# A gated attention block on one core: x loaded with its features in the partitions, norm factors spread by four transposes, first queries and keys tile by tile of u

## The chip, the cores and the metric

The kernel runs on one core of one Trainium2 chip. The metric is the device time of one execution in microseconds (us). PE stands for TensorE, DVE for VectorE, ACT for ScalarE, POOL for GpSimd and SP for SyncE, as in the profile; line numbers such as L157 are those of the kernel before, if nothing else is said.

## What is computed

One layer of a block with three branches on x (512 tokens, 1024 features), with 256 memory tokens and a feed-forward part of 4096 columns, all float32:

```
u = rmsnorm(x, g_mix)
proj = u @ w_in          # GLA q,k,v,out-gate,alpha | FoX q,k,v,forget | memory query | 3 gates
y_gla, y_fox, y_mem = three attentions, each through its output matrix
h = x + (sig(g0)*y_gla + sig(g1)*y_fox + sig(g2)*y_mem) @ w_out
h = h + square(relu(rmsnorm(h, g_ffn) @ w_ff1)) @ w_ff2
out = rmsnorm(h, g_final)
rmsnorm(x, g): x * rsqrt(mean(x*x over the features) + 1e-6) * g
mk, mv = split(rmsnorm(mem, g_mem) @ w_mem_kv)
```

u is needed with its features in the partitions: 8 tiles of 128 features by 512 tokens. The mean runs over the features.

## The kernel before

Every factor of a product is split in two parts, a high one (`whi`, `uhi`: the value cast to a rounded 32-bit type) and a low one (`wlo`, `ulo`: what the cast left off), and a product is three matmuls: high by high, high by low, low by high (`mm3`, L157 to L159). The weights lie in DRAM as chunks of 128 x 1024 (512 KB). For a chunk, SP issues the load into one of three buffers `raw`, ACT casts it to `whi` (L147), DVE subtracts to get `wlo` (L148), in `split_w`; `whi` and `wlo` have three buffers each as well. PE runs in the order of the program text. What ACT, DVE, POOL and SP do is put in order by a scheduler when the kernel is built, within what explicit "after" relations leave open; once built, each engine runs its instructions strictly in that order.

POOL issues two kinds of DMA that matter here. `next_sum` (L122) counts the calls of `split_w`; from the 12th call on it issues with each call one step that makes sums of weight chunks in DRAM (tiles `T`: copies at L133, adding transfers at L131), and each step waits for the cast of its call. The two gate projections of the second half (`gate_group`) work on sums of weight chunks too: `wb` buffers are loaded by SP, and a second chunk is added by a POOL DMA (`plus`, L1032); then ACT casts the buffer (L147), DVE takes the low part (L148), and eight groups of three matmuls on 128x256 follow (`product`). `take` brings the product out of PSUM: for number 5 it is an ACT copy into `ct` (L1062).

The front, before the change: x comes as four tiles of 128 tokens by 1024 features (`xn`). For each, ACT squares it with a running sum (L330), DVE and POOL make the norm factor (L333, and a power of -0.5 on POOL, L334), and DVE scales the tile (L340). PE has meanwhile computed the memory keys (L380) and half of the memory values (`mem_values`, L394). It then transposes x, 32 blocks of 128x128 (L408), eight blocks of four at a time into PSUM, with the rest of the memory values between them. ACT makes `uhi` (L411) and DVE `ulo` (L412) of each tile, both from PSUM. After it come `g_proj` (L504/L505, the projection with the alpha and forget columns, 16 matmuls) and `fox_pair(0)`: the first 128 query columns (24 matmuls) and then the first 128 key columns (24 matmuls), whose `ulo` and low weights are all there by then.

Of the kernel before, what the change touches and what calls it, by code (L numbers as in the profile page):

```python
# [9 lines left out]
F32 = mybir.dt.float32  # L10
# [7 lines left out]
P = 128  # L18
D = 1024
S = 512  # L20
# [12 lines left out]
def chunk_list():  # L33

    L = []
    for c in (0, 512):
        L += [("N", "w_mem_kv", 2 * j, c) for j in range(4)]
    L += [("G",)]
    L += [("T", "w_in", OFF["fq"]), ("T", "w_in", OFF["fk"])]
# [24 lines left out]
def hybrid_block(ctx, tc, chunks, wst, memT, xN, gffn, gfin, wup, cst, out):  # L64
# [57 lines left out]
    def next_sum(after):  # L122
# [5 lines left out]
        for to, src, add_ in islice(sums[len(late_on)], 1 + (len(late_on) == 1)):  # L128
            with tc.issue_after(merged[0]) if late_on else ExitStack():
                if add_:  # L130
                    d = nc.gpsimd.dma_start(to, src, accum_op=ALU.add, max_dma_last_dim=8192)  # L131
                else:
                    d = nc.gpsimd.dma_start(to, src)  # L133
            tc.add_manual_dep(d.ins, after.name, mybir.DependencyInfo(mybir.DependencyClass.Sync, mybir.DependencyReason.DATA),
                              reason="pace")

# [116 lines left out]
    with pool("front") as fp:  # L253
# [4 lines left out]
        xn = fp.tile([P, NT, D], F32, name="xn")  # L258
        ssx = small(fp, NT, "ssx")
# [61 lines left out]
        load, act, vec = next(lead(chunks[4], after=(load, act, vec)))  # L321

        def x_load(t):
            with behind(load):
                return nc.sync.dma_start(xn[:, t, :], xN[t * P:(t + 1) * P, :]).ins

        def x_square(t):
            sq = fp.tile([P, D], F32, tag="xsq", name=nm("xsq"), bufs=2)
            with behind(act):
                a = nc.scalar.activation(sq, xn[:, t, :], AF.Square, accum_out=ssx[:, t:t + 1]).ins  # L330
            ms, r = (fp.tile([P, 1], F32, tag=g, name=nm(g), bufs=2) for g in ("ms", "rr"))
            with behind(vec):
                m = nc.vector.tensor_scalar(ms, ssx[:, t:t + 1], 1.0 / D, EPS, op0=ALU.mult, op1=ALU.add).ins  # L333
            nc.gpsimd.tensor_tensor(r, ms, mhalf[:, :1], op=ALU.pow)  # L334
            return a, m, r

        def x_scale(t, r, cols=(0, D)):
            for sl in (slice(a, b) for a, b in zip(cols, cols[1:])):
                with behind(vec):
                    v = nc.vector.tensor_scalar(xn[:, t, sl], xn[:, t, sl], r, None, op0=ALU.mult).ins  # L340
            return v

        for t in range(2):
            load = x_load(t)
            act, vec, r = x_square(t)
            if t == 0:
                vec = x_scale(t, r)
        load, act, vec = next(lead(chunks[5], after=(load, act, vec)))
        load = x_load(2)
        act, vec, r2 = x_square(2)  # L350
        vec = x_scale(1, r)
        vec = x_scale(2, r2)
        load = x_load(3)
        act, vec, r = x_square(3)
        x_scale(3, r, (0, 2 * P, D))
        x_act = act
        with behind(load):
            nc.sync.dma_start(ident, cst[:, :P])
        get_plain = get_w

        def get_first(key):
            return pre[key] if key in pre else get_plain(key)

        get_w = get_first
# [18 lines left out]
        def mem_values():  # L383
            pss = [at_() for _ in range(2)]
            for j in range(4):
                with behind(u_mid if j == 3 else None):
                    w = [x.rearrange("p (k c) -> p k c", k=2) for x in get_w(("N", "w_mem_kv", 2 * j, 512))]
                for low in range(2):
                    for t, ps in enumerate(pss):
# [6 lines left out]
                        if j == 3 and low:  # L396
                            with tc.issue_after(u_end):
                                nc.vector.tensor_copy(gqT[t], ps)
                        yield

        def k_copies(after, hs):
            with tc.issue_after(after):
                for h in hs:
                    nc.scalar.copy(mk_raw(h), kps[h])

        def turn(pt, k, ts):
            for t in ts:
                nc.tensor.transpose(pt[:, t * P:(t + 1) * P], xn[:, t, k * P:(k + 1) * P], ident)  # L408

        def u_split(pt, k):  # L410
            a = nc.scalar.mul(uhi[:, k, :], pt, gmix[:, k:k + 1]).ins  # L411
            return a, nc.vector.scalar_tensor_tensor(ulo[:, k, :], pt, gmix[:, k:k + 1], f(uhi[:, k, :]), op0=ALU.mult,  # L412
                                                  op1=ALU.subtract).ins
# [3 lines left out]
        k_copies(x_act, (0, 1))  # L417
        mv = mem_values()
        macc, rm, dg = gv[:, 2, :M], gv[:, 1, :2], gv[:, 3, :M]
        msq = [fp.tile([P, 4, M], F32, name=f"msq{h}") for h in range(2)]  # L420
        u_act = None
        run(islice(mv, 8))
        pts, u_mid = [at_() for _ in range(2)], None
        for ts in (range(NT - 1), (NT - 1,)):
            for k in range(2):
                turn(pts[k], k, ts)
        for k in range(KT):
            if k > 1:
                pts.append(at_())
                turn(pts[k], k, range(NT))  # L430
            u_act, u_end = u_split(pts[k], k)
            u_mid = u_act if k == 3 else u_mid
            u_late = u_act if k <= 5 else u_late
            if k in (1, 3, 5):
                run(islice(mv, 2))
            if k in (5, 7):
                h = k // 7
                with tc.issue_after(u_act):
                    nc.scalar.activation(msq[h], memr[:, 4 * h:4 * h + 4, :], AF.Square)
        k_copies(u_act, (2, 3))  # L440
        run(mv)
        hold[0] = u_late
        get_w = get_plain
        g_raw = wp.tile([P, 1024], F32, tag="raw", name=nm("raw"))
        with tc.issue_after(nc.sync.dma_start(g_raw, wst[index["G",]]).ins):
            nc.sync.dma_start(cst_s[:, P:5 * P], cst[:, P:5 * P])
            nc.sync.dma_start(wup_s, wup)
            nc.sync.dma_start(cmask, cst[:, 5 * P:])

        with tc.issue_after(u_end):  # L450
            nc.vector.tensor_copy(msk_s.rearrange("p a b -> p (a b)"), cst_s[:, 3 * P:5 * P])
            nc.vector.tensor_tensor(msq[0], msq[0], msq[1], op=ALU.add)
            nc.vector.tensor_tensor(msq[0][:, :2, :], msq[0][:, :2, :], msq[0][:, 2:, :], op=ALU.add)
            nc.vector.tensor_tensor(macc, msq[0][:, 0, :], msq[0][:, 1, :], op=ALU.add)
# [31 lines left out]
    with pool("fox") as xp:  # L486
        gaT = xp.tile([P, S], F32, tag="oT", name="gaT")
        def ga_evac(ps):
            nc.scalar.copy(gaT, ps)
            nc.vector.memset(gaT[32:33, :], 1.0)  # L490
# [4 lines left out]
        def g_proj():  # L495

            raw = g_raw.rearrange("p (k c) -> p k c", k=KT)
            w = wp.tile([P, 1024], F32R, tag="hi", name=nm("whi")).rearrange("p (k c) -> p k c", k=KT)
            with tc.issue_after(hold[0]):
                nc.scalar.copy(w, raw)  # L500
            nc.vector.tensor_tensor(w[:, :, 64:], raw[:, :, 64:], f(w[:, :, 64:]), op=ALU.subtract)
# [6 lines left out]
        g_proj()  # L508
# [58 lines left out]
        def fox_pair(j):  # L567
# [12 lines left out]
            yield from proj(OFF["fq"] + P * j, q_evac)  # L580
            yield from proj(OFF["fk"] + P * j, k_evac)
# [104 lines left out]
        run(fox_pair(0))  # L686
# [581 lines left out]
    with pool("ff") as yp:  # L1268
# [51 lines left out]
        @contextmanager  # L1320
        def in_order():

            traced = nc.cur_bb.bb.instructions
            last, behind = traced[-1], {}
            yield
            for i in traced[next(k for k in reversed(range(len(traced))) if traced[k] is last) + 1:]:
                if i.engine in (mybir.EngineType.DVE, mybir.EngineType.Activation, mybir.EngineType.SP):
                    if i.engine in behind:
                        tc.add_manual_dep(i, behind[i.engine].name, mybir.DependencyInfo(
                            mybir.DependencyClass.NoSync, mybir.DependencyReason.DATA), reason="order")  # L1330
                    behind[i.engine] = i

# [360 lines left out]
def layout(inputs):  # L1693
# [39 lines left out]
    def tl(a):  # L1733
# [26 lines left out]
        "wst": wst, "memT": mem_flat, "xN": np.ascontiguousarray(x),  # L1760
# [27 lines left out]
```

## Time and profile before

| | |
|---|---|
| median of 3 runs | 815.94 us (815.68 to 816.97) |
| profiled execution | 815.5 us, of which the profiled span is 813.7 us |
| granted TensorE clock, mean | 0.997 |
| PE busy | 803.3 us (99%) |
| DVE, ACT, POOL busy | 591.3, 442.0, 109.0 us |

The span runs from the first to the last instruction that the profiler saw; 1.8 us of the profiled execution's time lie outside it. In the lists, a row has the start in us, the duration in us, the engine, the line, the operation, output <- inputs, the size, and in brackets how long the engine had been idle and what released it. "x2" is a row of two instructions of one kind, which the duration spans.

### The profile page before, as it was taken

Reading aid. Unit: us, or ns where it says so; the run is one execution under the profiler, and the core shown is the slowest. Engines: PE = TensorE matmul, PEld = TensorE weight load, DVE = VectorE, ACT = ScalarE, POOL = GpSimd, SP = SyncE. Lnnn points to the kernel's source line nnn. Section 1 sums busy time; section 2 is a strip of 40 time slices with the busy share of each in tenths; the row PEclk is TensorE's granted clock in tenths of the full one; section 3 lists DMA queues with packets and bytes.
Section 4 is the critical chain, followed back from the end, with each engine's and each line's share of the span. In section 5 each row is a group of like instructions: output and inputs, shape, how many; then the busy total and the mean of one; then the engine's idle time right before and its main releaser. Section 6 shows DMA issues by size and latency. Waiting matters only on the chain.

```text
span 813.7 us, 12505 instructions
## 1 busy us (share of the span) xinstructions
PE 803.3 (99%) x4813; PEld 706.9 (87%) x4813; DVE 591.3 (73%) x913; ACT 442.0 (54%) x699; POOL 109.0 (13%) x135
## 2 busy tenths in 40 slices
PE   8999999999999999999999999999999999999996
PEld 7788888888888888999999889987998899889984
DVE  5856878546455587877567468788788778887896
ACT  7745655543344334444454346874676367637764
POOL 0000110011101112134144110011001100100011
PEclk9999999999999999999999999999999999999998
DMA  9534666688888877767768733998758966896643
GB/s 354 168 118 139 190 177 200 184 236 200 252 236 273 232 227 184 170 165 196 199 148 225 247 98 130 279 233 232 239 163 200 222 210 167 194 281 193 160 82 125
DMA packets 39484, 161.29 MB, mean 198 GB/s; under 512 B 4736, under 2 KB 5184, under 8 KB 37056
## 3 DMA queue, kind: packets, MB, share of 16 engines
q0 software_dynamic: 9776, 58.20, 34.3%
q1 hardware_dynamic: 27856, 97.55, 34.1%
q10 hardware_dynamic: 1792, 4.75, 1.7%
q8 instruction: 37, 0.61, 0.3%
q14 instruction: 23, 0.19, 0.1%
HBM read 158.35 MB, written 35.68 MB: 238 GB/s over the span
## 4 chain that ended last, share of the span: by engine, by line
PE 92%; DVE 3%; ACT 2%; DMA 2%; issue 1%; POOL 0%; POOLq 0%; DVEq 0%; ACTq 0%
PE mm L1233 18%; PE mm L157 17%; PE mm L158 17%; PE mm L159 17%; PE a L157 5%; PE a L158 4%; PE a L159 4%; PE mm L380 1%; PE a L394 1%; DMA b<-in_wst_dram 1%; ACT hi L1357 1%; DVE lo L1291 1%; PE a L624 1%; DVE h L1285 1%; PE a L662 1%
## 5 line engine op out<-in xcount | busy, mean ns | idle before, releaser
L148 DVE TENSOR_TENSOR wlo<-raw,whi 128x1024 fp32r<-128x1024 f32 x65 | 84.1, 1296 | 58.4 <-ACT whi L147 58.2
L157 PE MATMUL mm<-uhi,whi 128*128 128x512 f32 (+1 forms) x352 | 125.8, 357 | 0.0
L159 PE MATMUL mm<-uhi,wlo 128*128 128x512 f32 (+1 forms) x352 | 123.7, 351 | 0.0
L158 PE MATMUL mm<-ulo,whi 128*128 128x512 f32 (+1 forms) x352 | 123.6, 351 | 0.0
L147 ACT CAST whi<-raw 128x1024 fp32r<-128x1024 f32 x65 | 68.4, 1052 | 89.2 <-PE mm L158 54.4
L1289 ACT CAST hi<-raw 128x1024 fp32r<-128x1024 f32 x56 | 58.8, 1050 | 45.1 <-PE mm L1233 30.2
L1291 DVE TENSOR_TENSOR lo<-raw,hi 128x1024 fp32r<-128x1024 f32 x56 | 68.5, 1223 | 14.6 <-ACT hi L1289 14.6
L157 PEld LDWEIGHTS mm<-uhi,whi 128*128 128x128 f32 x352 | 66.7, 189 | 9.9 <-issue 1.5
L159 PEld LDWEIGHTS mm<-uhi,wlo 128*128 128x128 f32 x352 | 66.6, 189 | 9.1
L158 PEld LDWEIGHTS mm<-ulo,whi 128*128 128x128 f32 x352 | 66.7, 189 | 8.1
L1233 PE MATMUL mm<-u2l,hi 128*128 128x256 f32 x240 | 66.1, 283 | 0.0
L1233 PE MATMUL mm<-u2h,hi 128*128 128x256 f32 x240 | 66.1, 283 | 0.0
L1233 PE MATMUL mm<-u2h,lo 128*128 128x256 f32 x240 | 61.1, 283 | 0.0
L1643 POOL DMA_DIRECT2D b<-in_wst_dram x30 | 25.6, 854 | 264.2 <-DVE lo L1291 153.3
L1289 ACT CAST hi<-b 128x1024 fp32r<-128x1024 f32 x36 | 37.8, 1049 | 38.1 <-PE mm L159 24.0
L158 PE MATMUL mm<-lo,ch 128*128 128x512 f32 x136 | 53.0, 390 | 0.7 <-DVE lo L1291 0.7
L157 PE MATMUL mm<-hi,ch 128*128 128x512 f32 x136 | 52.9, 389 | 0.0
L159 PE MATMUL mm<-hi,cl 128*128 128x512 f32 x136 | 52.9, 389 | 0.0
L1233 PE MATMUL mm<-u2sh,hi 128*128 128x256 f32 x192 | 52.6, 283 | 0.0
L1233 PE MATMUL mm<-u2sl,hi 128*128 128x256 f32 x192 | 52.5, 283 | 0.0
L1291 DVE TENSOR_TENSOR lo<-b,hi 128x1024 fp32r<-128x1024 f32 x36 | 43.9, 1221 | 10.4 <-ACT hi L1289 10.2
L1233 PE MATMUL mm<-u2sh,lo 128*128 128x256 f32 x192 | 47.5, 283 | 0.0
(423 smaller groups left out, 2105.7 us busy)
## 6 DMA issues: line engine op xcount, KB each, us to landing
raw<-in_wst_dram SPq DMA_DIRECT2D x113, 512.0 KB
raw<-T SPq DMA_DIRECT2D x32, 512.0 KB
b<-in_wst_dram POOLq DMA_DIRECT2D x32, 512.0 KB, 5.6
T<-in_wst_dram POOLq DMA_DIRECT2D x12, 1024.0 KB, 9.0
b<-in_wst_dram SPq DMA_DIRECT2D x16, 512.0 KB
wb<-in_wst_dram POOLq DMA_DIRECT2D x15, 512.0 KB, 5.4
T<-in_wst_dram POOLq DMA_DIRECT2D x12, 512.0 KB, 5.7
wb<-in_wst_dram SPq DMA_DIRECT2D x8, 512.0 KB
```

The source lines that it names most:

```text
L147: cast = nc.scalar.copy(hi, raw)
L148: low_now[0] = nc.vector.tensor_tensor(lo, raw, f(hi), op=ALU.subtract).ins
L157: nc.tensor.matmul(ps, lh, rh, start=start, stop=False, skip_group_check=on)
L158: nc.tensor.matmul(ps, lh, rl, start=False, stop=False, skip_group_check=on)
L159: nc.tensor.matmul(ps, ll, rh, start=False, stop=stop, skip_group_check=on)
L380: nc.tensor.matmul(kps[h], w[:, h * P:(h + 1) * P], x[:, k, :], start=k == p == 0, stop=k == KT - 1 and p == 2)
L394: nc.tensor.matmul(ps, x[:, k, sl], w[low][:, kk, :], start=k == low == 0 and x is mxh, stop=k == KT - 1 and low == 1)
L624: nc.tensor.matmul(ps[e], q[a, sl], k[a, :w], start=p == 0, stop=p == 2)
L1233: nc.tensor.matmul(ps[:, a, :], x[:, a, k, :], y[:, s, k, :], start=start, stop=stop, skip_group_check=go is not None)
L1289: nc.scalar.copy(hi, raw)
L1291: nc.vector.tensor_tensor(lo, raw, f(hi), op=ALU.subtract)
L1643: nc.gpsimd.dma_start(to[i], wst[index["B", q, i, x]], accum_op=ALU.add)
```

## The change

- x is given a second layout in DRAM, `xT`: four pieces of 2 x 128 features by 512 tokens, so that SP loads it with the features in the partitions (`xt`). The 32 transposes go away.
- The squares are made on ACT from `xt` and added up over the eight feature tiles by DVE. Four matmuls with a column of ones sum over the partitions, giving the mean for 128 tokens each; one power on POOL makes all 512 factors (`rx`); four transposes, each of a column spread over 128 columns, put them as the same row in all partitions in PSUM (`rb`), and ACT copies that into SBUF (`rb_s`).
- The tiles of `xt` are multiplied by that row: tiles 0, 1 on DVE from `rb`, tiles 2 and 4 on DVE from `rb_s`, tiles 3, 5, 6, 7 on POOL from `rb_s`. `uhi` (ACT) and `ulo` (DVE) are made from `xt` in SBUF.
- The memory values come ahead of the first use of u. Then the first queries and keys go tile by tile of u: four matmuls for a tile (high weights of both by `uhi` and `ulo`), then `g_proj`, then the 16 matmuls of the low weights.
- The weights for them are loaded earlier (their order: the first queries, the first keys, then the chunk of `g_proj`), and they, like memory-value chunks 6 and 7, are split without a call of `next_sum`. The instructions of ACT, DVE and SP in the front are held in the order of the text (`in_order`, moved up in the file). The copies of the memory values to `gqT` go from DVE to ACT.

The core of the diff:

```diff
+        def x_square(j):
+            sq = fp.tile([P, 2, S], F32, tag="xsq", name=nm("xsq"), bufs=3)
+            for k in range(2) if j == 3 else [slice(0, 2)]:
+                nc.scalar.activation(sq[:, k], xt[:, 2 * j:2 * j + 2, :][:, k], AF.Square)
+            if j == 1:
+                nc.vector.tensor_tensor(sq, sq, sqs[0], op=ALU.add)
+            sqs.append(sq)
...
+        def lead_w(key, raw):
+            hi, lo = pre[key] = [wp.tile([P, 1024], F32R, tag=g, name=nm(g)) for g in ("hi", "lo")]
+            nc.scalar.copy(hi, raw)
+            return lambda: nc.vector.tensor_tensor(lo, raw, f(hi), op=ALU.subtract)
...
-        run(islice(mv, 8))
-        pts, u_mid = [at_() for _ in range(2)], None
-        for ts in (range(NT - 1), (NT - 1,)):
-            for k in range(2):
-                turn(pts[k], k, ts)
+        lead_w(chunks[6], vraws[0])()
+        run(islice(mv, 9))
+        ps = at_()
+        for t in range(NT):
+            nc.tensor.matmul(ps[:, t:t + 1], ssum[:, t * P:(t + 1) * P], ones[:, 0:1], start=True, stop=True)
+        nc.vector.tensor_scalar(ms, ps[:, :NT], 1.0 / D, EPS, op0=ALU.mult, op1=ALU.add)
+        nc.gpsimd.tensor_tensor(rx, ms, mhalf[:, :NT], op=ALU.pow)
+        lead_w(chunks[7], vraws[1])()
+        k_copies(range(4))
+        run(islice(mv, 3))
+        rb = at_()
+        for t in range(NT):
+            nc.tensor.transpose(rb[:, t * P:(t + 1) * P], rx[:, t:t + 1].to_broadcast([P, P]), ident)
+        lows = [lead_w(chunks[8 + n], fraws[n]) for n in range(2)]
+        def x_scale(k):
+            (nc.gpsimd if k in (3, 5, 6, 7) else nc.vector).tensor_tensor(xt[:, k, :], xt[:, k, :], rb_s if k > 1 else rb, op=ALU.mult)
+        def u_high(k):
+            nc.scalar.mul(uhi[:, k, :], xt[:, k, :], gmix[:, k:k + 1])
+        def u_low(k):
+            nc.vector.scalar_tensor_tensor(ulo[:, k, :], xt[:, k, :], gmix[:, k:k + 1], f(uhi[:, k, :]), op0=ALU.mult,
+                                           op1=ALU.subtract)
         for k in range(KT):
+            if k != 1:
+                x_scale(k)
+            u_high(k)
+            if k == 0:
+                x_scale(1)
+                nc.scalar.copy(rb_s, rb)
+            else:
+                u_low(k - 1)
...
+        def first_pair():
+            evacs = fox_pair(0)
+            ws = [[x.rearrange("p (k c) -> p k c", k=KT) for x in pre[chunks[n]]] for n in (8, 9)]
+            pss = [mmt() for _ in range(2)]
+            for k in range(KT):
+                for u in (uhi, ulo):
+                    for w, ps in zip(ws, pss):
+                        nc.tensor.matmul(ps, w[0][:, k, :], u[:, k, :], start=k == 0 and u is uhi, stop=False)
+            g_proj()
+            for w, ps, evac in zip(ws, pss, evacs):
+                for k in range(KT):
+                    nc.tensor.matmul(ps, w[1][:, k, :], uhi[:, k, :], start=False, stop=k == KT - 1)
+                evac(ps)
...
-        run(fox_pair(0))
+        first_pair()
```

How it moves instructions, at the places that the prediction speaks of. First DVE in the front, where u is made, before (`a_...` are the transposed tiles in PSUM, `wlo` low weights):

```order
L148 TENSOR_TENSOR wlo_406<-raw_403,whi_405 128x1024
L412 SCALAR_TENSOR_TENSOR ulo<-a_389,cols_s,uhi 128x512
L412 SCALAR_TENSOR_TENSOR ulo<-a_390,cols_s,uhi 128x512
L412 SCALAR_TENSOR_TENSOR ulo<-a_417,cols_s,uhi 128x512
L412 SCALAR_TENSOR_TENSOR ulo<-a_424,cols_s,uhi 128x512
L148 TENSOR_TENSOR wlo_452<-raw_449,whi_451 128x1024
```

and now (`a_419` is the row of factors in PSUM, `rb_s` its copy in SBUF; the lines are those of the changed file):

```order
L439 TENSOR_TENSOR xt<-xt,a_419 128x512 x2
L445 SCALAR_TENSOR_TENSOR ulo<-xt,cols_s,uhi 128x512
L439 TENSOR_TENSOR xt<-xt,rb_s 128x512
L445 SCALAR_TENSOR_TENSOR ulo<-xt,cols_s,uhi 128x512 x2
L439 TENSOR_TENSOR xt<-xt,rb_s 128x512
L445 SCALAR_TENSOR_TENSOR ulo<-xt,cols_s,uhi 128x512 x5
```

DVE used to read each tile of u from PSUM, with one input in SBUF beside it; now, but for the two tiles scaled by `a_419`, both large inputs of every instruction lie in SBUF, and four more multiplications of the kind of L439 stand on POOL in a row.

Second ACT in the first gate group, around 320 to 335 us of the span, before (`wb_3166` and `wb_3165` are the two weight buffers, `mm_3266` the product that `take` number 5 brings out, `f1h` the high part of another factor):

```order
L1057 COPY ct_3167<-mm_3177 128x2x256
L147 CAST whi_3262<-wb_3165 128x1024
L1044 ACTIVATE ct_3167<-ct_3167 128x2x256
L147 CAST whi_3297<-wb_3166 128x1024
L1014 CAST f1h_3161<-x_2990 128x1024
L1062 COPY ct_3168<-mm_3266 128x2x256
L147 CAST whi_3326<-wb_3165 128x1024
```

and now (`wb_3132` is what `wb_3166` was, `mm_3234` what `mm_3266` was):

```order
L1086 COPY ct_3133<-mm_3144 128x2x256
L160 CAST whi_3229<-wb_3131 128x1024
L1073 ACTIVATE ct_3133<-ct_3133 128x2x256
L1043 CAST f1h_3127<-x_2955 128x1024
L1091 COPY ct_3134<-mm_3234 128x2x256
L160 CAST whi_3265<-wb_3132 128x1024
L160 CAST whi_3295<-wb_3131 128x1024
```

The cast of the second weight buffer stood ahead of `f1h` and of the copy of a product; now it stands behind both. PE uses that buffer in the product that follows the copied one, as before.

Third POOL at the same place, before (`T_3_90` and `T_3_92` are sums in DRAM, `rr` the power for a norm of the GLA heads):

```order
L131 DMA T_3_90<-in_wst_dram 128x2048
L852 MEMSET ex_2837 128x8
L133 DMA T_3_92<-T_3_90 16x16384
L131 DMA T_3_92<-in_wst_dram 128x2048
L217 TENSOR_TENSOR rr_3044<-ms_3043,mhalf 128x4
L217 TENSOR_TENSOR rr_3057<-ms_3056,mhalf 128x4
L1032 DMA wb_3166<-in_wst_dram 128x1024
L1032 DMA wb_3165<-in_wst_dram 128x1024 x2
```

and now:

```order
L133 DMA T_3_90<-T_3_89 16x16384
L230 TENSOR_TENSOR rr_3022<-ms_3021,mhalf 128x4
L131 DMA T_3_90<-in_wst_dram 128x2048
L1061 DMA wb_3132<-in_wst_dram 128x1024
L1061 DMA wb_3131<-in_wst_dram 128x1024
L133 DMA T_3_92<-T_3_90 16x16384
L1061 DMA wb_3131<-in_wst_dram 128x1024
```

Four calls of `next_sum` fewer come ahead, so each sum step waits for the cast of a later call, and the steps of `T_3_90` and `T_3_92` now stand between and around the second `rr` and the `wb` transfers. On PE the rows behind the front are the same as before, in the same order.

More of the change, by code (lines that the diff above doesn't have):

```diff
@@ L320, in hybrid_block @@
         nc.gpsimd.tensor_copy(cols_s, mem_s[:, KT * M:])
[L321 to L364, printed above, removed]
+        order = in_order()
+        order.__enter__()
@@ new lines, in x_sum @@
+        def x_sum(j, k):
+            nc.vector.tensor_tensor(sqs[1][:, 0], sqs[1][:, 0], sqs[j][:, k], op=ALU.add)
+        for j in range(2):
+            x_load(j)
+            x_square(j)
+        next(lead(chunks[5]))
+        for j in range(2, 4):
+            x_load(j)
+        vraws = [fp.tile([P, 1024], F32, tag="lead", name=nm("raw"), bufs=2) for _ in range(2)]
+        nc.sync.dma_start(vraws[0], wst[6])
+        nc.sync.dma_start(ident, cst[:, :P])
+        nc.sync.dma_start(vraws[1], wst[7])
@@ L396, in mem_values @@
                         if j == 3 and low:
-                            with tc.issue_after(u_end):
-                                nc.vector.tensor_copy(gqT[t], ps)
+                            nc.scalar.copy(gqT[t], ps)
                         yield
[L401 to L408, printed above, removed]
@@ L440, in hybrid_block @@
-        k_copies(u_act, (2, 3))
-        run(mv)
[L442 to L454, printed above, removed]
+        ms, rx = (small(fp, NT, g) for g in ("ms", "rx"))
@@ L495, in g_proj @@
         def g_proj():
[L497 to L501, printed above, removed]
+            w = gw3
             ps = mmt()
@@ L1318, in late_left @@
             left(i, 3, s1[i])
[L1320 to L1331, printed above, removed]
         U2.update({5: (u2s, 0), 6: (u2s, 1), 7: (u2s, 2)})
```

85 lines of the change are left out of this document (55 added, 30 removed).

## The prediction, made before the changed kernel was run

> **What bounds the kernel now.** I read the page first, then the busy time by stretches, then the chain of work that ended last, cut to its first 100 us, then single rows.
>
> ```profile
> span 813.7 us, 12505 instructions
> PE 803.3 (99%) x4813; PEld 706.9 (87%) x4813; DVE 591.3 (73%) x913; ACT 442.0 (54%) x699; POOL 109.0 (13%) x135
> ```
>
> PE is busy 803.3 of 813.7 us. The stretches (PE's busy time is the second number, the clock, DMA share and GB/s the last three) say where the other 10.4 lie:
>
> ```profile
> 10.00:20.00 10.00, 10.00 (x76) 9.49 (x75) 7.01 (x13) 7.91 (x13) 1.11 (x2) 1.00 1.03 407
> 20.00:30.00 10.00, 9.99 (x54) 7.56 (x53) 7.48 (x12) 7.62 (x14) 1.49 (x2) 1.00 0.52 188
> 160.00:800.00 640.00, 639.20 (x3933) 571.38 (x3932) 471.20 (x616) 338.88 (x487) 95.30 (x108) 1.00 0.74 201
> ```
>
> In the front and from 160 to 800 us PE hardly ever waits (0.8 us in 640), at full clock. So work taken off PE is gained in full, no wait is left to be removed there, and any new wait of PE is lost in full. The chain in the front:
>
> ```profile
> by line: PE mm L157 17.9%; PE mm L158 17.3%; PE mm L159 17.1%; PE mm L380 11.8%; PE a L394 11.2%; PE a L408 4.3%; DMA mem_s<-in_memT_dram 4.0%; PE a L624 2.8%; PE mm L504 1.8%; PE mm L505 1.8%; PE a L520 1.8%; PE mm L624 1.7%; PE a L645 0.9
> 5.79 11.78 PE mm L380 x96
> 17.57 5.62 PE a L394 x24
> 23.19 0.87 PE a L408 x8
> 33.14 0.23 PE mm L504
> ```
>
> From 5.79 us on it is PE alone: keys, half of the values (5.62/24 = 0.234 us a matmul), then transposes and values in turn, `g_proj` from 33.14.
>
> **The change, part by part: PE's work.** The 32 transposes are 4.3% of the 100 us that this chain covers: 4.3 us (the six pieces add up to 4.32, of which the first is the x8 above). In their place stand four transposes, 4 x 0.87/8 = 0.44, and four matmuls of one column. A matmul of that kind is in the trace:
>
> ```profile
> 67.07 0.34 PE a L460 x4
> ```
>
> Those are two of the program's (each shows as two records), so four take 0.68. The matmuls of the first queries and keys keep their number. Sum: -4.32 + 0.44 + 0.68 = **-3.20 us**. It is nearly the whole gain that the change can have.
>
> **The feed of the front.** PE reaches the sums of squares at about 24.1 (the 24 values, then four more), the transposes at 26.7, and with the remaining values (0.234 each, 12 of them) the first tile of u at 29.94 (17.57 + 48 x 0.234 + 0.68 + 0.44). What must be ready for that:
>
> ```profile
> 20.49 1.06 ACT L330 ACTIVATE xsq<-xn 128x1024 f32<-128x1024 f32 x1 [0.16 <-DMA xn<-in_xN_dram]
> L217 POOL TENSOR_TENSOR rr<-ms,mhalf x4: 1005/1034/1842, 284.6 to 313.2; 128x4 f32<-128x4 f32 x4
> 42.98 0.58 ACT L489 COPY gaT<-mm 128x512 f32<-128x512 f32 x1
> ```
>
> The last piece of x lands at 20.5 now, and the DMA engines are full until then (share 1.03 from 10 to 20 us). At 407 GB/s a chunk takes 1.3 us, so chunks 6, 7, queries, keys and `g_proj` come at about 21.7, 23.1, 24.4, 25.7, 27, each ahead of its first use. Squares of 1.06 and additions of 0.7 on DVE end near 22.9. The power on 128x4 took 1.0 to 1.84 us; at 1.0 the factors stand at about 26.2, at 1.84 they are late by up to 0.5. I cost the feed at **0**; the ends are 0 (an earlier finish gains nothing, PE still has its values to do) and +1.0. ACT's copy of the row (as the copy above, 0.58) puts `rb_s` at about 29.2, 28.0 + 0.65 for the first `uhi` + 0.55.
>
> **DVE and POOL in turn.** From then on a tile needs a multiplication, `uhi` and `ulo`. PE takes four matmuls a tile, at the pitch of these rows (21 steps in 4.76 us: 0.2267 each, 0.907 a tile):
>
> ```profile
> 53.82 0.39 PE L159 MATMUL mm<-whi,ulo 128*128 128x512 f32 x1
> 58.58 0.39 PE L159 MATMUL mm<-whi,ulo 128*128 128x512 f32 x1
> ```
>
> It asks for `ulo` of tile 3 at 29.94 + 3 x 0.907 + 2 x 0.2267 = 33.1. Alone, DVE needs 0.65 an instruction and POOL 1.25 (below), which would nearly keep up. But rows in which both work on SBUF together read otherwise. POOL and DVE at 413 us, then each kind alone:
>
> ```profile
> 413.35 3.85 POOL L1089 TENSOR_TENSOR acc<-acc,ct 128x512 f32<-128x512 f32 x2 [2.69 <-DVE ct L1088]
> 414.32 1.72 DVE L148 TENSOR_TENSOR wlo<-raw,whi 128x1024 fp32r<-128x1024 f32 x1
> 415.97 1.78 DVE L1093 SCALAR_TENSOR_TENSOR ml<-acc,mh 128x512 fp32r<-128x512 f32 x1
> 439.07 2.55 POOL L1089 TENSOR_TENSOR acc<-acc,ct 128x512 f32<-128x512 f32 x2 [9.71 <-DVE ct L1088]
> L1291 DVE TENSOR_TENSOR lo<-raw,hi 128x1024 fp32r<-128x1024 f32 x56 | 68.5, 1223 | 14.6 <-ACT hi L1289 14.6
> L1282 DVE TENSOR_TENSOR s<-ev,od 128x512 f32<-128x512 f32 x8 | 5.5, 692 | 0.0
> ```
>
> Alone the two POOL additions take 2.55, the DVE instructions 1.22 and 0.69 (in a row some 0.08 less each, since they overlap at their ends). Together they run from 413.35 to 417.75, that is 4.40 us, where 2.55 + 1.22 + 0.69 = 4.46. The two engines did not work side by side at all; they took turns, instruction by instruction. In the changed front four POOL multiplications (5.0 us) and, until `ulo` of tile 3 is done, five DVE instructions on SBUF pairs (two multiplications, `ulo` of tiles 1, 2, 3: 3.25) go through that gate from 29.2 on: 29.2 + 8.25 = 37.5. Where the turns fall doesn't change this sum. PE waits in all until 37.55 rather than 33.1: **+4.5 us**. Behind that, `ulo` comes every 0.65 and PE takes 0.907 a tile, so no more is lost. The bounds: +0.8 if they don't block each other (DVE's seven instructions from 28.0 to `ulo` of tile 3 make 4.6, and two waits for `uhi` of 0.65 bring that to 33.9), +4.7 with 1.30 for POOL's; I take 4.5, since the rows show turns. In the kernel before, `uhi` and `ulo` read PSUM,
>
> ```profile
> 28.83 1.35 ACT L411 ACTIVATE uhi<-a,cols_s 128x512 fp32r<-128x512 f32 x2
> 30.07 1.40 DVE L412 SCALAR_TENSOR_TENSOR ulo<-a,cols_s,uhi 128x512 fp32r<-128x512 f32 x2
> ```
>
> and POOL has no work of 512 columns in the front, so this wait is new. The Trainium skill, "SBUF — State Buffer", section "Who interferes with whom", says what speaks against this change: a DVE instruction with two SBUF inputs contends with a GpSimd instruction that reads SBUF, and the one that issues later is held off entirely. The trace agrees with the turns. The same page (section "A bandwidth-pool intuition that's wrong (but worth ruling out)") gives some 115 ns more at a handover, measured on descriptors; with eight handovers the estimate by that page would be a wait of about 5.4 us instead. The 4.40 us above show no such gap, so it stays out.
>
> **The first gate group.** Behind the front the order of PE is the same; on ACT one cast has moved behind a copy that waits for PE. The rows of before around it:
>
> ```profile
> 328.79 1.06 ACT L147 CAST whi<-wb 128x1024 fp32r<-128x1024 f32 x1 [2.37 <-DMA wb<-in_wst_dram]
> ...
> 333.00 0.59 ACT L1062 COPY ct<-mm 128x512 f32<-128x512 f32 x1 [2.21 <-PE mm L159]
> 333.48 1.05 ACT L147 CAST whi<-wb 128x1024 fp32r<-128x1024 f32 x1
> 332.68 0.28 PE L159 MATMUL mm<-f0h,wlo 128*128 128x256 f32 x1
> 333.04 0.28 PE L159 MATMUL mm<-uhi,wlo 128*128 128x256 f32 x1
> 334.56 1.23 DVE L148 TENSOR_TENSOR wlo<-wb,whi 128x1024 fp32r<-128x1024 f32 x1 [2.32 <-ACT whi L147]
> ```
>
> The product with `f0h` ends with the matmul of 332.68; the copy of it starts at 333.00. The next product (`uhi` by the second buffer) starts 0.12 after and asks for its `wlo` at 333.04, which was there, since the cast was done at 328.79. Now the cast comes after the copy: it runs from 333.48 to 334.53, `wlo` (1.23) until 335.8, so the matmul of 333.04 runs at 335.8: **+2.8 us**. Queued behind the cast is the cast of the other buffer (1.05), needed only after this product, 24 matmuls on; it follows in the shadow. No row hides this wait, since the copy can't start before the product that it copies ends, and PE goes from that product straight to the next. Its lower end is +2.6 (copy, cast and subtraction without a gap, from 333.48: 0.97 + 1.15), its upper end hangs on the transfer that adds to the buffer:
>
> ```profile
> DMA to landing us min/median/max: 5.1/8.5/11.4
> 313.22 1.84 POOL L217 TENSOR_TENSOR rr<-ms,mhalf 128x4 f32<-128x4 f32 x1 [1.39 <-DVE ms L216]
> 315.81 1.01 PE L932 MATMUL a<-cst_s,on 128*128 128x128 f32 x4
> ```
>
> The first of these lines is that of the adding sum transfers of L131. One of them (`T_3_90`) now waits for the cast of 319.5 and is issued just ahead of the buffer's own. If the buffer's landing is put off behind it, it stands at about 332.6, which the cast just meets; at the longest, 11.4, up to 336, for a wait of 6. I take 2.8. Of the rest, the copy of `T_3_90` (about 0.5 on POOL) stands between the two powers and puts the second off by some **0.35**; PE uses it at 315.81, just in time now (0 to 0.4). The other sum steps come later as well, each by the time of some four casts; I know of no reader near them and take 0.
>
> **The sum.** -3.20 + 0 + 4.5 + 2.8 + 0.35 = +4.45 on the profiled execution, 815.5 + 4.45 = 819.95. The median of the runs shown is 0.44 above that execution, so 820.4.
>
> **The rivals.** A, not slower: DVE and POOL work side by side in the front. Place: the stretch from 29 to 38 us; price: 4.5 falls to 0.8; it decides by whether a DVE row beside a POOL row there keeps 0.65 us. Sum: -3.20 + 0.8 + 2.8 + 0.35 = +0.75, 816.7, within a measurement's reach of no change. For it: the only rows of turns are additions, these are multiplications with one operand shared. Against: every pair of rows in the trace that overlaps shows turns.
> B, faster: neither wait reaches PE, -3.20 + 0.35, 813.1. It needs `ulo` of tile 3 by 33.1, and the moved cast started by 330.7 (333.04 less 1.05 and 1.23), which is 2.8 us before the copy ahead of it can start; against it stands the bracket "[2.21 <-PE mm L159]" of that copy.
> C, slower still: the adding transfers of the buffers land late, so that the gate group waits some 3 us more, there or at its next buffers: 823.5. For it: landings of the sum transfers go up to 11.4. Against: the DMA share from 160 us on is 0.74.
>
> **How the numbers follow.** Forecast 0.62, at 820.4 (own range 818.5 to 821.5). A 0.20, B 0.08, C 0.10. A measurement of this kernel can tell 0.2% (1.6 us) from no change. Slower is the forecast and C: 0.72; within 0.2%, A: 0.20; faster, B: 0.08. The range of 815.2 to 824.2 holds the forecast, A and the nearer part of C with the bounds of the terms, and leaves out B.
>
> **What would show it.** In the changed profile: no L408 and 3.2 us less of PE before the first use of u; DVE rows of multiplication or `ulo` near 1.9 us beside POOL rows from 29 on, and PE idle some 4.5 us until about 38, released by DVE; at the gate a hole of 2.8 us in PE, released by DVE `wlo`, with the ACT copy ahead of the cast. It would be wrong if DVE rows there stay at 0.65, if PE starts the first tile later than 31 for want of the factors (the feed), or if the gate's hole is filled.

## The result, and the profile after

The changed kernel takes 823.0 us in the median of six runs (821.39 to 825.98), the kernel before 816.89 (815.68 to 817.35) beside it: 1.0081 times as long, 95% interval 1.0061 to 1.0102. It is slower, by about 6.6 us. The prediction said 820.4 in a range of 815.2 to 824.2. The direction and both places of the loss were right. The median lies outside the forecast's own range of 818.5 to 821.5: the sum had no term for matmuls at half clock, and it took the work saved on PE 1 us too large. The profiled execution took 822.19 us with a span of 820.4, 6.7 more than before.

The page of the changed kernel:

```profile
span 820.4 us, 12462 instructions
PE 804.9 (98%) x4793; PEld 707.4 (86%) x4793; DVE 598.9 (73%) x913; ACT 443.9 (54%) x699; POOL 113.5 (14%) x136
```

PE has 20 records fewer and is busy 1.6 us longer: part of its work ran slower. The busy time by stretches says where (PE's is the second number, its clock the third from the end):

```profile
30.00:40.00 10.00, 7.61 (x26) 5.03 (x25) 9.88 (x10) 5.79 (x10) 6.43 (x4) 0.83 0.00 1
...
160.00:330.00 170.00, 170.00 (x934) 143.77 (x933) 104.09 (x175) 67.27 (x122) 24.10 (x36) 1.00 0.80 228
330.00:345.00 15.00, 12.08 (x77) 11.28 (x76) 9.08 (x9) 6.18 (x7) 3.73 (x5) 0.89 0.91 230
345.00:800.00 455.00, 454.47 (x2915) 415.04 (x2914) 354.73 (x425) 263.37 (x355) 68.39 (x71) 1.00 0.73 196
```

There are two places: 2.4 us of holes and a clock of 0.83 from 30 to 40, and 2.9 us of holes and 0.89 from 330 to 345. Elsewhere PE is as full as before, but for 0.31 us at 27. Since PE's order behind the front is unchanged, each of its matmuls can be set beside its counterpart of before, and the difference of their starts is how far the kernel is behind at that point:

| matmul | before | after | behind by |
|---|---|---|---|
| first of the memory keys | 5.79 | 5.88 | 0.09 |
| alpha columns, first of the common order | 47.50 | 49.74 | 2.24 |
| last row of the product by `f0h`, gate group 1 | 332.68 | 334.94 | 2.26 |
| first low-weight matmul of the next product | 333.04 | 338.65 | 5.61 |
| last of that product | 335.56 | 342.76 | 7.20 |
| MLP, after an older wait | 551.29 | 557.95 | 6.66 |

**The front.** DVE and POOL, then PE, in the changed kernel:

```profile
30.18 1.78 DVE L439 TENSOR_TENSOR xt<-xt,rb_s 128x512 f32<-128x512 f32 x1
31.89 3.44 DVE L445 SCALAR_TENSOR_TENSOR ulo<-xt,cols_s,uhi 128x512 fp32r<-128x512 f32 x2
35.25 1.76 DVE L439 TENSOR_TENSOR xt<-xt,rb_s 128x512 f32<-128x512 f32 x1
36.94 3.61 DVE L445 SCALAR_TENSOR_TENSOR ulo<-xt,cols_s,uhi 128x512 fp32r<-128x512 f32 x5
30.03 6.43 POOL L439 TENSOR_TENSOR xt<-xt,rb_s 128x512 f32<-128x512 f32 x4 [2.80 <-ACT rb_s L454]
```

```profile
27.28 0.65 PE L435 MATMUL a<-cst_s,rx 128*128 128x128 f32 x4 [0.31 <-POOL rx L429]
...
33.70 0.73 PE L605 MATMUL mm<-ulo,hi 128*128 128x512 f32 x2 [1.57 <-DVE ulo L445]
...
35.38 1.17 PE L605 MATMUL mm<-ulo,hi 128*128 128x512 f32 x2 [0.49 <-DVE ulo L445]
36.36 1.05 PE L605 MATMUL mm<-uhi,hi 128*128 128x512 f32 x2
37.73 1.22 PE L605 MATMUL mm<-ulo,hi 128*128 128x512 f32 x2 [0.32 <-DVE ulo L445]
```

As long as POOL's four multiplications run (until 36.46), each DVE instruction takes 1.7 to 1.8 us; the five in the row of 36.94, behind it, take about 0.75 each. PE waits for `ulo` three times, and gets tile 3's at 37.7, where 37.55 was predicted. The pairs that took 0.62 take 1.05 to 1.22 from 35.4 to 38.7: that is the clock (0.57 on average from 35 to 39 us), of which more below.

**The gate group.** ACT, POOL and PE of the changed kernel, and the line on the transfer issued at 325.46:

```profile
335.26 0.59 ACT L1091 COPY ct<-mm 128x512 f32<-128x512 f32 x1 [2.56 <-PE mm L172]
336.29 1.04 ACT L160 CAST whi<-wb 128x1024 fp32r<-128x1024 f32 x1 [0.44 <-DMA wb<-in_wst_dram]
323.07 0.88 POOL L131 DMA_DIRECT2D T<-in_wst_dram  x1 [5.71 <-ACT whi L160]
325.46 0.89 POOL L1061 DMA_DIRECT2D wb<-in_wst_dram  x1 [1.51 <-DVE wb L1070]
...
DMA to landing us min/median/max: 10.8/10.8/10.8
```

```profile
337.39 0.39 PE L170 MATMUL mm<-uhi,whi 128*128 128x256 f32 x1 [2.16 <-ACT whi L160]
...
338.65 0.39 PE L172 MATMUL mm<-uhi,wlo 128*128 128x256 f32 x1 [0.76 <-DVE wlo L161]
...
339.83 0.41 PE L170 MATMUL mm<-uhi,whi 128*128 128x256 f32 x1
340.04 0.41 PE L171 MATMUL mm<-ulo,whi 128*128 128x256 f32 x1
```

The cast stands behind the copy, as the order said; but the copy was done at 335.85, and then the cast waited 0.44 us more for the buffer, whose adding transfer took 10.8 us to land (5.5 before), behind the sum transfer of 323.07 (the line `T`). So two causes end within half a microsecond here, and the trace alone can't say what either is worth. From about 339.4 the matmuls come every 0.213 us instead of 0.12, at a granted clock of 0.50 from 340 to 342 us: half clock.

### The profile page after: what moved, and what is told of

Same layout as the page of the kernel before. It is cut to its first block, busy times and chain, and to the rows that moved or that the text cites. A ratio compares the mean times of both kernels' runs of the same rounds, so it can differ in the third digit from the quotient of the medians.

```text
span 820.4 us, 12462 instructions
## 1 busy us (share of the span) xinstructions
PE 804.9 (98%) x4793; PEld 707.4 (86%) x4793; DVE 598.9 (73%) x913; ACT 443.9 (54%) x699; POOL 113.5 (14%) x136
## 4 chain that ended last, share of the span: by engine, by line
PE 89%; DVE 4%; DMA 3%; ACT 2%; issue 1%; POOL 0%; POOLq 0%; DVEq 0%; ACTq 0%
PE mm L1262 18%; PE mm L170 16%; PE mm L172 16%; PE mm L171 16%; PE a L170 4%; PE a L171 4%; PE a L172 4%; PE mm L388 1%; DMA wb<-in_wst_dram 1%; DMA b<-in_wst_dram 1%; PE a L401 1%; ACT hi L1373 1%; DVE lo L1320 1%; PE a L653 1%; PE a L691 1%
## 5 line engine op out<-in xcount | busy, mean ns | idle before, releaser
L170 PE MATMUL mm<-uhi,whi 128*128 128x512 f32 (+1 forms) x336 | 120.5, 359 | 2.2 <-ACT whi L160 2.2
L172 PE MATMUL mm<-uhi,wlo 128*128 128x512 f32 (+1 forms) x336 | 118.2, 352 | 0.8 <-DVE wlo L161 0.8
L171 PE MATMUL mm<-ulo,whi 128*128 128x512 f32 (+1 forms) x336 | 118.0, 351 | 0.0
L161 DVE TENSOR_TENSOR wlo<-raw,whi 128x1024 fp32r<-128x1024 f32 x61 | 79.7, 1311 | 51.7 <-ACT whi L160 51.5
L160 ACT CAST whi<-raw 128x1024 fp32r<-128x1024 f32 x61 | 63.9, 1051 | 80.1 <-PE mm L171 50.1
L170 PEld LDWEIGHTS mm<-uhi,whi 128*128 128x128 f32 x336 | 64.4, 192 | 11.6 <-ACT whi L160 2.4
L172 PEld LDWEIGHTS mm<-uhi,wlo 128*128 128x128 f32 x336 | 64.3, 191 | 9.5 <-DVE wlo L161 1.0
L171 PEld LDWEIGHTS mm<-ulo,whi 128*128 128x128 f32 x336 | 64.5, 192 | 7.5
```

The lines of the kernel that those rows point to most:

```text
L160: cast = nc.scalar.copy(hi, raw)
L161: low_now[0] = nc.vector.tensor_tensor(lo, raw, f(hi), op=ALU.subtract).ins
L170: nc.tensor.matmul(ps, lh, rh, start=start, stop=False, skip_group_check=on)
L171: nc.tensor.matmul(ps, lh, rl, start=False, stop=False, skip_group_check=on)
L172: nc.tensor.matmul(ps, ll, rh, start=False, stop=stop, skip_group_check=on)
```

## The experiments

Each kernel's ratio is to the kernel before, run beside it, with its 95% interval. "Behind" is always PE's place against the profile of the kernel before, as in the table above. The theory: DVE and POOL take turns in the front, and at the gate group the order on ACT makes PE wait. The rivals: in the front, the feed is slow without turns; at the gate, it is the late landing of the buffer.

### Undoing the later sums

`chunk_n` holds the count of calls of `next_sum`; it starts four higher:

```diff
-    late_on, merged, chunk_n, ... = [], [None], [0], ...
+    late_on, merged, chunk_n, ... = [], [None], [4], ...
```

> The changed kernel with the count of casts started four higher, so that each sum step in DRAM waits for the same cast as before the change; on ACT the moved cast stands ahead of the copy again. If the gate group's wait came from this shift (by the order on ACT, by the late landing, or by both), PE's holes at 335 us and the half clock behind them (4.6 us of offset from 2.24 to 6.9) go away: about 818.4 in the median, 0.2 to 0.3% over the kernel before. If the wait there has another cause (the front's delay carried on), the time stays near 823.

Measured: 816.97 us, ratio 1.0006 (0.9995 to 1.0017), 1.4 us under what was expected. PE at the gate group:

```profile
330.00:345.00 15.00, 15.00 (x102) 13.71 (x101) 12.05 (x12) 6.80 (x8) 2.60 (x3) 1.00 0.67 132
```

So the whole gate loss came from four calls of a counter, which the change in the front made fewer by splitting four weight chunks in another helper. Every `T` step shifts by four casts, and with the steps both the landing and ACT's order. What is left of the change, with the front as it is, is no difference that can be told.

The expected time had carried over the front of one profiled execution, with its half clock. Of the twelve executions here, five show a mean granted clock of 0.994 to 0.996 and took 816.5 to 819.1 us; seven show 0.997 or 0.998 and took 815.8 to 817.3. The profiled one is the longest of all. Its PE leaves the front 3.15 us behind, which is more than the median execution loses in all; what the front costs in the median is not shown by any trace.

### The order alone

On top of that kernel, the copy of product 5 is put ahead of the cast of the second buffer:

```diff
                 with tc.issue_after(cast):
-                    take(5, p5)
-                p7 = product(7, split_w(other))
+                    c5 = nc.scalar.copy(c22, p5).ins
+                with tc.issue_after(c5):
+                    w7 = split_w(other)
+                p7 = product(7, w7)
```

> The kernel of e3_pace with one cast of the second weight buffer moved behind the copy of product 5 on ACT, and nothing else moved on any engine: the order alone, with the transfers early. If the order costs what was predicted, PE waits 2.8 us at the gate group and then runs some us at half clock (1.5 us): 4.3 us over e3_pace. If only the late landing made the wait, it equals e3_pace within 0.5 us.

Measured: 821.73 us, ratio 1.0066 (1.0047 to 1.0085), 4.8 us over the kernel above. ACT in this kernel:

```profile
334.93 0.59 ACT L1152 COPY ct<-mm 128x512 f32<-128x512 f32 x1 [2.56 <-PE mm L172]
335.41 1.99 ACT L160 CAST whi<-wb 128x1024 fp32r<-128x1024 f32 x2
```

```profile
337.77 0.58 PE L172 MATMUL mm<-uhi,wlo 128*128 128x256 f32 x1 [0.76 <-DVE wlo L161]
```

The buffer was there (no DMA in the brackets), and the cast followed the copy at once. PE fell back by 2.8 us at the matmul that was at 333.04 before (from 1.93 to 4.73 us behind), the number that was predicted, and by another 1.4 in the half clock behind it.

### The late landing alone

The changed kernel, with the cast put back ahead of the copy, and the sums late:

```diff
-                with tc.issue_after(cast):
+                w7 = split_w(other)
+                with tc.issue_after(cast_now[0]):
                     take(5, p5)
-                p7 = product(7, split_w(other))
+                p7 = product(7, w7)
```

> The changed kernel with that cast put back ahead of the copy on ACT, but the sum steps as late as the change has them: the late landing alone. If the order made the wait, the gate group's 3.4 us and the clock's 1.6 us go: about 818. If the landing at 336.3 holds the cast anyway (it ended 0.44 us behind the copy in the profile), nothing is gained: within 1 us of the changed kernel, about 822.5.

Measured: 824.12 us, ratio 1.0093 (1.0075 to 1.011): nothing gained. ACT:

```profile
337.81 1.04 ACT L160 CAST whi<-wb 128x1024 fp32r<-128x1024 f32 x1 [3.84 <-DMA wb<-in_wst_dram]
```

The cast, free of the copy, waits 3.84 us for a transfer that took 11.0 to land. PE falls back by 3.6 us at the matmul of 333.04 and by 2.2 more at half clock. Each cause is enough for the loss by itself; taking one away bares the other.

### The later sums without the new front

The kernel before, with the counter started at -4:

> The kernel before the change with one number changed: the count of casts starts four lower, so that every sum step in DRAM waits for a cast four later; the front is untouched. If the late sums make the gate group's wait by themselves (landing behind a sum transfer, and a cast behind a copy on ACT), it takes 3.4 us of wait and 1.5 us of half clock there: about 821. If the wait also needed the new front's delay, it stays near 816.5.

Measured: 821.12 us, ratio 1.0066 (1.0047 to 1.0085). The gate's loss needs nothing of the front: it is nearly as large in a kernel whose front is that of before (2.96 us behind at the matmul of 333.04, 4.5 after the half clock).

```profile
336.00 0.58 PE L159 MATMUL mm<-uhi,wlo 128*128 128x256 f32 x1 [0.76 <-DVE wlo L148]
```

### One transfer moved behind

The kernel of the late landing, with the last three sum steps two casts later still:

```diff
-        if n <= 11:
+        if n <= 11 or n in (41, 42):
             return
```

> The kernel of e5_landing (cast ahead of the copy, late sums) with the last three sum steps of that series, the adding transfer of T_3_90 first, two casts later still, so that it is issued behind the first two adding transfers of the weight buffers instead of just ahead of them; the copy of T_3_90 stays ahead. If the buffer landed late because it was queued behind that one transfer, it lands some 6 us after its issue instead of 11, the hole at 337 us and its half clock go, and the time is about 819 (what is left is the front's 2 to 3 us). If it was late because the late sums load the DMA engines in general, nothing changes: 824.

Measured: 826.85 us, ratio 1.0122 (1.0098 to 1.0145): the time went the wrong way for both readings. ACT at the first gate group and at the second:

```profile
331.18 1.05 ACT L160 CAST whi<-wb 128x1024 fp32r<-128x1024 f32 x1 [2.40 <-DMA wb<-in_wst_dram]
...
365.58 1.04 ACT L160 CAST whi<-wb 128x1024 fp32r<-128x1024 f32 x1 [11.34 <-DMA wb<-in_wst_dram]
```

At the first group the landing went back from 11.0 to 5.5 us, and PE has no hole there (still 2.3 us behind at 344). But the steps that were moved now stand ahead of the next group's buffer: a sum transfer issued at 352.51, the buffer's at 353.06, which took 12.4 us to land, and PE waited 5.3 us at 366. The late landing goes with the sum transfer issued just ahead, at both places: the buffer lands 3.3 us after the sum transfer in the changed kernel and 4.0 us after it here. Whether it stands behind that transfer or shares the DMA engines with it, no run tells. That the moved transfers would meet the next buffer was not seen ahead.

### All multiplications on DVE

```diff
-            (nc.gpsimd if k in (3, 5, 6, 7) else nc.vector).tensor_tensor(xt[:, k, :], xt[:, k, :], rb_s if k > 1 else rb, op=ALU.mult)
+            nc.vector.tensor_tensor(xt[:, k, :], xt[:, k, :], rb, op=ALU.mult)
...
-                nc.scalar.copy(rb_s, rb)
```

> The changed kernel with all eight multiplications on DVE, reading the row of factors from PSUM; POOL does none, and ACT makes no copy of the row. If DVE and POOL take turns, DVE's rows fall from 1.7 to 0.65 us, sixteen of them end about 38.5 where PE wants the last at 37.4, and PE loses about 1.1 us in the front instead of 4.7: 3.5 us less than the changed kernel, about 819.5. If the DVE rows are slow by themselves and POOL did work beside them, the four multiplications that DVE takes over come on top: 2 us or more slower than the changed kernel, 825.

Measured: 820.59 us, ratio 1.005 (1.0033 to 1.0067). One of DVE's rows:

```profile
31.37 0.68 DVE L439 TENSOR_TENSOR xt<-xt,a 128x512 f32<-128x512 f32 x1
```

With more work on DVE the front is faster: every row takes 0.68 or 0.75, and the front ends 0.82 us ahead of the kernel before instead of 2.24 behind it. Of these 3.1 us the run gained some 2.5 (0.3% by the ratios). In its profile, the longest of its six executions (822.53 us), PE comes to 470 us earlier than in the changed kernel and waits there for casts of weights whose load came late:

```profile
473.80 0.49 PE L170 MATMUL mm<-whi,mh 128*128 128x512 f32 x1 [0.52 <-ACT whi L160]
475.85 0.75 PE L171 MATMUL mm<-wlo,mh 128*128 128x512 f32 x1 [1.56 <-DVE wlo L161]
```

With the counter at 4 as well:

> e1_dve_scale and e3_pace together: all multiplications on DVE from PSUM, and the sum steps as early as before the change. If the offset of e1_dve_scale's front, 0.85 us under the kernel before, is what the front gives, and all that came later (4 us at 335, 3 us at 470) was from the late sums, the time is about 815.6, 0.1% under the kernel before. If the holes at 335 and 470 have causes of their own, it stays over 818.

Measured: 814.46 us, ratio 0.9978 (0.9966 to 0.9989). PE is full at 335 and at 470, and 0.8 us ahead at both. So the holes at 470 came from the late sums too.

### The same instructions, another place of one input

On top of the kernel with the sums put back, DVE's two multiplications of tiles 2 and 4 read the row from PSUM; POOL keeps its four, and no instruction moves:

```diff
-            (...).tensor_tensor(xt[:, k, :], xt[:, k, :], rb_s if k > 1 else rb, op=ALU.mult)
+            (...).tensor_tensor(xt[:, k, :], xt[:, k, :], rb_s if k in (3, 5, 6, 7) else rb, op=ALU.mult)
```

> The kernel of e3_pace with the two multiplications of tiles 2 and 4 on DVE reading the row of factors from PSUM instead of its copy in SBUF; the order of all engines is unchanged. If only DVE instructions with two inputs in SBUF wait for POOL, these two rows fall from 1.7 to 0.68 us and stand beside POOL's, ulo of tile 3 comes about 1.2 us earlier, and the time is about 1 us under e3_pace: 816.0. If any DVE instruction waits for POOL, it equals e3_pace, 817.0.

Measured: 815.12 us, ratio 0.9986 (0.9976 to 0.9996): by the ratios 0.2%, 1.6 us, under the kernel with the row in SBUF. DVE, with POOL under way from 29.96 to 36.43:

```profile
30.11 0.68 DVE L439 TENSOR_TENSOR xt<-xt,a 128x512 f32<-128x512 f32 x1
30.71 2.89 DVE L445 SCALAR_TENSOR_TENSOR ulo<-xt,cols_s,uhi 128x512 fp32r<-128x512 f32 x2
33.52 0.67 DVE L439 TENSOR_TENSOR xt<-xt,a 128x512 f32<-128x512 f32 x1
```

The multiplications with one input in PSUM take 0.68 and 0.67 beside POOL; those with both in SBUF took 1.78 and 1.76 at the same places, and `ulo`, with both in SBUF, still waits. It is the place of the inputs that makes the turns. The kernel before had shown as much, beside the POOL additions of 413.35 that the prediction reads; `a` is in PSUM:

```profile
413.73 0.68 DVE L1088 SCALAR_TENSOR_TENSOR ct<-ct,a 128x512 f32<-128x512 f32 x1
```

The gain is more than the 1 us forecast; in this profile PE's three holes of 0.5 us left the clock at 1.00, where it fell to 0.90 from 30 to 40 us in the profile of `e3_pace`, with the row in SBUF.

### A front without the waits

On top of `e7_dve_pace`, the order of the front is changed (the core of it):

```diff
         for k in range(KT):
-            if k != 1:
-                x_scale(k)
+            x_scale(k)
             u_high(k)
...
+        for k in range(KT):
+            u_low(k)
...
+            main(uhi, range(KT))
+            main(ulo, range(3))
+            gps = mmt()
+            for k in range(KT):
+                nc.tensor.matmul(gps, gw3[:, k, :], uhi[:, k, :], start=k == 0, stop=False)
+            main(ulo, range(3, KT))
```

> The kernel of e7_dve_pace with the front put in another order: DVE makes all eight multiplications first and the low parts after them, PE takes the high parts of all tiles, then the low parts of three tiles, then g_proj by the high parts, and the other low parts. The mechanism: PE's need of low parts comes later than DVE's sixteen instructions of 0.65. If nothing but those waits kept the 3.2 us of transposes from being gained, PE loses 0.6 us at most in the front and the offset there is 1.8 to 2.3 us under the kernel before: about 814.4. If the feed ahead of it (factors, weights) is the limit, it equals e7_dve_pace.

Measured: 813.45 us, ratio 0.996 (0.9945 to 0.9975): it beats both kernels, the one before by 2.4 us in the medians and 3.3 by the ratio. PE, where each row is a run without a break:

```profile
30.30 3.98 PE L600 MATMUL mm<-uhi,hi 128*128 128x512 f32 x16
34.12 1.55 PE L600 MATMUL mm<-ulo,hi 128*128 128x512 f32 x6
35.51 1.98 PE L606 MATMUL mm<-uhi,whi 128*128 128x512 f32 x8
37.33 2.43 PE L600 MATMUL mm<-ulo,hi 128*128 128x512 f32 x10
```

The front has no hole behind the transposes, and the alpha columns come 2.47 us ahead of the kernel before. 0.23 of that is an earlier start of the keys (5.56 against 5.79), so the work saved is 2.24. At 469 us PE waits 0.4 us for a low weight, and 1.9 us of the lead stay.

### The clock behind a hole

The kernels of `e3_pace` and `e4_order` have the same front, and in their profiles the same three holes (1.6, 0.5 and 1.2 us from 32 to 38). Then, first in the one and then in the other:

```profile
38.00:39.00 1.00, 1.00 (x4) 0.78 (x3) 1.00 (x3) 1.00 (x3) 0.00 (x0) 0.53 0.00 0
39.00:40.00 1.00, 1.00 (x4) 0.74 (x3) 1.00 (x3) 1.00 (x3) 0.00 (x0) 0.50 0.02 8
```

```profile
38.00:39.00 1.00, 1.00 (x5) 0.79 (x6) 0.99 (x2) 1.00 (x2) 0.00 (x0) 1.00 0.00 0
39.00:40.00 1.00, 1.00 (x6) 0.83 (x6) 1.00 (x2) 1.00 (x3) 0.00 (x0) 1.00 0.02 8
```

The one ran at half clock until 41.5 and was 3.15 us behind at 49, the other 1.9. So the same holes cost 1.2 us more in one execution than in another. In the five profiles with this front (these two, the changed kernel, `e5_landing` and `e9_behind`) PE was 1.9 to 3.5 us behind at its end. At the gate group all five profiles with the hole (2.4 to 2.9 us in all) show a clock below 0.9 from 330 to 345.

How long the half clock lasts can be reckoned from the mean clock of a stretch around it: 0.57 over 4 us is 3.4 us at half. At the gate of the changed kernel, and at that of `e5_landing`:

```profile
339.00:343.00 4.00, 4.00 (x24) 4.00 (x23) 3.11 (x3) 1.86 (x3) 1.58 (x3) 0.57 0.41 135
338.00:346.00 8.00, 6.64 (x31) 6.34 (x32) 5.86 (x5) 4.28 (x5) 2.63 (x3) 0.57 0.85 252
```

That is 3.4 us in the one and 6.9, twice as long, in the other; each of the other stretches at half clock behind the holes told here comes to one of these two lengths as well. The executions without a profile show the price only in their mean clock: the six of the changed kernel go from 821.39 us at 0.995 to 825.98 at 0.989, and all 30 of `e2_psum_rb`, `e6_front` and `e7_dve_pace`, whose profiles have no hole above 0.5 us from 20 to 50 us and none at the gate, lie at 0.997 or 0.998.

The Trainium skill, "TensorE: Matmul & The Clock Gate", section "Part 1: The HAM clock gate (the "warmup" mystery)", tells of a half rate decided over windows of some 3.4 us that run freely, so that the phase decides; the lengths and the change from execution to execution agree with the rows. By its table the half rate comes after at least one idle window; the rows differ from that, for here it came behind holes of 2.2 and 0.8 us at the gate, and behind 1.6, 0.5 and 1.2 us in the front.

## Why the prediction was right, and where not

| step | predicted | measured |
|---|---|---|
| PE's work, and the feed | -3.20, and 0 | -2.24 |
| front, DVE and POOL in turn | +4.5 | +4.4 |
| the second power | +0.35 | 0.0 |
| gate group, the wait | +2.8 | +3.4 |
| half clock behind it | none | +1.6 |
| later | 0 | -0.5 |

The measured column, with 0.09 of a later start, adds up to the 6.7 between the spans. The measured -2.24 is that of the front without holes (`e6_front`); the front's +4.4 is 2.24 - 0.09 + 2.24. The column is of one execution of each kernel. By the ratios, which are of all of them, the late sums cost more and the front less: putting the sums back takes off 0.75%, 6.1 us (`e3_pace`), and the late sums alone add 0.66%, 5.4 us (`e8_before_late`).

- **PE's work**: too large by 1 us. The four sums took 0.80 instead of 0.68, the transposes some 0.65 instead of 0.44, and the power took 1.88 us (the slow end, not the value taken), for which PE waited 0.31. The remaining 0.3 isn't assigned to a row.
- **Turns in the front**: right in mechanism, and shown three ways: by the rows, by taking POOL out, by moving one input to PSUM. They hold for instructions with both inputs in SBUF; that every pair of rows that overlaps shows turns was read too widely (413.73, above). The size is right in this profile, in part by luck. POOL's instructions took about 1.1 us between DVE's, not 1.25, and the row of factors came 0.8 us later than reckoned; these offset each other, and part of the 4.4 is matmuls at half clock: in `e4_order`, whose front ran at full clock, the same sum gives 4.05.
- **The second power**: no loss. PE is 2.24 us behind ahead of 315 and after it; the power took 1.29 us there instead of 1.84, which made up for the transfer issued ahead of it.
- **The gate group**: the order's price of 2.8 was exact where it was alone. In the changed kernel it wasn't what ended last. The prediction had the landing as "the cast just meets" it at 332.6, and in its rival C as a chance of 0.10; at 10.8 us it ended the wait, about half a microsecond later than the order would have.
- **The half clock** was missing from the sum: 1.6 us at the gate, and in the front between nothing and 1.6 us (`e4_order` against `e5_landing`, 1.9 and 3.5 behind). It is the step that failed: the forecast took a hole in PE to cost its own length only.
- **Rivals**: A, side by side, is refuted by the rows of 1.7 us; B did not occur (the moved cast was 2.8 us too late for it, as said, but the copy only 2.3: 333.00 less 330.7); C was true in its mechanism, and 823.5 is near the time measured, but by luck: the late landing added about half a microsecond to what the order costs, not 3 us, and the half clock made up the rest.

## What to carry to other kernels

Look at where the inputs of a DVE instruction lie before giving POOL a share of its work: here 0.68 us an instruction became 1.78 as soon as both engines read SBUF pairs, and giving DVE all the work, from PSUM, was faster than sharing it. When an edit changes how often a helper with a counter is called, follow what the counter paces: four calls moved DMAs and a cast 300 us away and cost 5.4 us by themselves, most of the loss. And where PE is 99% busy, price a hole of two microseconds or more as longer than itself (here by 1.4 to 2.2 us at the gate), and test two causes that end together by removing each and both.

## What the runs showed of the hardware

- A DVE instruction with both tensor inputs in SBUF and a POOL one with two inputs in SBUF exclude each other: 1.78 us for one of 0.68. With one input in PSUM it took 0.68 beside POOL.
- A buffer's adding transfer from POOL (320 to 372 us) landed in 5.1 to 7.0 us in the kernels with the early sums, and in 10.5 to 12.4 when a sum transfer of 1 MB was issued up to 2.4 us ahead of it on the same engine.
- After holes of PE of 2.4 to 2.9 us at the gate, its matmuls of 256 columns came every 0.213 us instead of 0.12, for 3.4 us in four profiles and 6.9 in a fifth, beginning up to two microseconds after it went on. Behind the front's three holes (1.6, 0.5 and 1.2 us) the half clock came in some executions and not in others; behind three of 0.5 us it did not come.
